# A mixture of experts on one core: gathers three experts ahead, hidden transposes ahead of the down products, second blocks turned and multiplied last

## The chip, the cores and the metric

The kernel runs on one core of a Trainium2 chip. The metric is the time of one execution on the device in microseconds (us); the time before is the median of 3 runs. A trace of one execution tells what each engine did: TensorE (PE; its weight loads are PEld), VectorE (DVE), ScalarE (ACT), GpSimd (POOL) and SyncE (SP), which issues the weight loads.

## The reference

The block is one decoder layer: a mixer (state space and pooling branches), then a mixture of experts over 512 tokens of width 1024, and a final norm. The change is in the experts. Each token picks 8 of 64 experts; each expert is a gated unit of width 256; a shared expert is added. Cut to what matters:

```python
u = modulate(rmsnorm(h), sh2, sc2)                      # 512 x 1024, float32
top_e, wts = routed(sigmoid(u @ w_router))              # 8 experts and weights for each token
for e in range(64):                                     # tokens of e in blocks of 128
    xb = u[tokens_of(e)]
    hid = silu(xb @ we_gate[e]) * (xb @ we_up[e])       # 1024 -> 256
    routed[tokens_of(e)] += (hid @ we_down[e]) * w      # 256 -> 1024
h = h + g2 * (routed + shared)
return rmsnorm(h, final_norm_g)
```

## The kernel before, in words

The expert stage (`experts`) is one loop over 64 experts, unrolled. How many tokens an expert has is known only at run time, so each engine loads the counts into registers and branches. There are three kinds. A light expert (up to 64 tokens, `LIGHT`) uses the float32 weights as they are. A heavy one (65 to 128) splits its weights into a high and a low float32r part (`split`, lines 45 and 46: a ScalarE cast to `wh` and a VectorE subtraction to `wl`) and makes three products for each (lines 61 to 63, `mm3`). An expert with over 128 tokens has a second block, worked like a heavy one. `by_count` chooses light or heavy, `if_heavy` runs a body for heavy ones, `if_two` for those with a second block. A branch is a unit for the semaphores: who waits for something written in a branch waits for the end of that branch on the engine.

For expert e the work is spread over several iterations:

- Index: `onehot` (line 851, VectorE) and `slot_product` (line 858, `ixp`, TensorE) make the token list of expert e + 4; `slot_numbers` reads it out.
- Rows: `fetch` and `fetch_over` gather the token rows into `xg` by an indirect DMA that GpSimd issues (line 885); `scatter` (line 1044) adds the results into `Y` in the same way.
- Turn: `turn_in` transposes gathered rows by TensorE into the two buffers `xt` (line 899); `turn_out` copies them out as a high part `xh` (line 909, ScalarE) and a low part `xl` (line 910, VectorE); a light expert has one copy, `xf`.
- Products: `products` makes gate and up into `gu` (lines 61 to 63, light: 976) and then `hid` (line 999 on VectorE, light: 1185 on ScalarE).
- Hidden: `hidden_in` transposes `hid` into `ht` (line 1008); `hidden_out` copies it out as `hh` (1014) and `hl` (1015); light: `hT`.
- Down: `downs` multiplies by the down weights into the two buffers `yo` (lines 61 to 63, light: 985) and copies to `yl` (1040, light: 988). It runs one iteration late: iteration e has the down products of e - 1.

The loop stands under `manual_schedule`: on each engine the instructions run in the order in which the code is written. In iteration e that is: gathers for e + 2; split of the first weight half of e + 1 (`gu0w`); products of e; products of its second block, if any (`second_products`); transposes of e + 1 (`turns`, `turned`), and in `turned`, for a heavy e + 1, the split of its second weight half (`gu1w`); the transposes of the second block of e + 1 (`next_second`); down products of e - 1; hidden of e; hidden and down products of the second block of e (`second_down`); scatters; weight loads for e + 2. The eight weight buffers are used in a ring, so a load waits on SyncE until a buffer's last reader is through; for the second half and the down weights of e + 2 that is the down product of e - 1.

Of the kernel before, what the change touches and what calls it, by code (L numbers as in the profile page):

```python
# [11 lines left out]
F32 = mybir.dt.float32  # L12
# [11 lines left out]
NT = 4  # L24
# [827 lines left out]
    return oh  # L852


def slot_product(k, ps, oh, vv, b):

    for t in range(NT):
        k.nc.tensor.matmul(ps[:, b, 0:5], oh[:, t, b, :], vv[:, t, :], start=t == 0, stop=t == NT - 1)


# [41 lines left out]
def turn_out(k, halves, x, full=None):  # L902

    nc = k.nc
    for hf, pv in enumerate(halves):
        ks = slice(hf * 4, hf * 4 + 4)
        if full is not None:
            nc.scalar.copy(full[:, ks, :], pv)
        nc.scalar.copy(x[0][:, ks, :], pv)  # L909
        nc.vector.tensor_sub(x[1][:, ks, :], pv, x[0][:, ks, :].bitcast(F32))  # L910
    return x


def turn(k, src, x, full=None):
    halves = turn_tiles(k)
    turn_in(k, src, halves)
    return turn_out(k, halves, x, full)
# [157 lines left out]
def experts(k, shared):  # L1075
# [79 lines left out]
    def by_count(e, engines, light, heavy):  # L1155

        if e == 0:
            heavy()
        elif e < E:
            with tc.If(count(e, engines) <= LIGHT) as small:  # L1160
                light()
            with small.Else():
                heavy()
# [32 lines left out]
    def turned(e, halves):  # L1196

        if e == E:
            return
        def light():  # L1200
            for hf, pv in enumerate(halves):
                nc.scalar.copy(k.xf[:, hf * 4:hf * 4 + 4, :], pv[:, :, :LIGHT])

        def heavy():
            turn_out(k, halves, k.xT[e % 2])
            gu[e][1].split(k, k.gu1w)

        by_count(e, both, light, heavy)

    def downs(e):  # L1210
        if e < 0:
# [6 lines left out]

        by_count(e, every, lambda: down_light(k, k.hT, dn[e], y, w), heavy)

    def hidden_turned(e, hid):
        ps = hidden_in(k, hid)

        def light():
            nc.scalar.activation(k.hT, ps[:, :, :LIGHT], AF.Silu)
            nc.vector.tensor_mul(k.hT, k.hT, ps[:, :, LIGHT:])  # L1226

        by_count(e, both, light, lambda: hidden_out(k, ps, k.hx[e % 2]))

    with tc.manual_schedule():  # L1230
        fetch_over(0)
        fetch_over(1)
        if_two(0, lambda: turn(k, k.xg[3], k.xT[1]))
        for e in range(E):
            fetch(e + 2)
            fetch_over(e + 2)
            onehot(e + 4)
            for i in (e, e + 1):
                if i < E:
                    for engines in (every, both):  # L1240
                        count(i, engines)
            if_heavy(e + 1, both, lambda: gu[e + 1][0].split(k, k.gu0w[(e + 1) % 2]))
            hid = products(e)
            hid1, halves = hidden(k), turn_tiles(k)
            slots = slot_tile(k, 2) if e + 4 < E else None

            def turns():
                if e + 1 < E:
                    turn_in(k, xg[e + 1], halves)

            def second_products():
                gate_act(k, gate_up_mm(k, k.xT[(e + 1) % 2], gu[e]), hid1)
                turns()

            def index_part(b):
                if e + 4 < E:
                    slot_product(k, slots, oh[e + 4], k.V[:, :, e + 4, :], b)

            def next_second():
                index_part(0)  # L1260
                turn(k, k.xg[3 + (e + 1) % 2], k.xT[e % 2])

            def second_down():
                ps = turn_tiles(k)[0].rearrange("p q t -> p (q t)")[:, :2 * P].rearrange("p (j t) -> p j t", j=2)
                hidden_in(k, hid1, ps)
                index_part(1)
                hidden_out(k, ps, k.hx[2])
                for n in range(2):
                    down(k, k.hx[2], dn[e], n, k.xg[2], idx[e][1][:, 1:2])

            if_two(e, second_products, turns)
            turned(e + 1, halves)
            if_two(e + 1, next_second, lambda: index_part(0))
            downs(e - 1)
            hidden_turned(e, hid)
            if_two(e, second_down, lambda: index_part(1))
            if e > 0:
                first(e - 1, lambda n: scatter(k, idx[e - 1], 0, k.yl[(e - 1) % 2], (e - 1) % 2, n))
            second(e, lambda n: scatter(k, idx[e], 1, k.xg[2], e % 2, n))
            load(e + 2)  # L1280
            if e + 4 < E:
                idx[e + 4] = slot_numbers(k, slots, 2)
        e = E - 1
        downs(e)
        first(e, lambda n: scatter(k, idx[e], 0, k.yl[e % 2], 1, n))
        part = k.part = [token_pair(k, k.Y[0], t) for t in (0, 2)]
        for t in range(NT):
            eng = (nc.vector, nc.gpsimd)[t % 2]
            y, h = (u[t // 2][:, t % 2, :] for u in (part, k.hs2))
            eng.tensor_mul(y, y, k.rows[:, 0, :])  # L1290
            eng.tensor_add(h, h, y)  # L1291
# [183 lines left out]
```

## Time and profile before

| what | value |
|---|---|
| median of 3 runs | 1673.15 us (1671.15 to 1684.17) |
| the profiled execution's own time | 1673.0 us |
| its span, first to last instruction | 1671.3 us |
| mean granted TensorE clock, share of full | 0.947 |
| TensorE busy, share of the span | 88% |
| VectorE, ScalarE, GpSimd | 61%, 45%, 22% |
| HBM traffic over the span | 206 GB/s |

Busy is what an engine's instructions cover; a wait is idle time ahead of an instruction, put down to what ended it. "ACTq" or "DVEq" is a sequencer of that engine that signals without work, for instance in passing a branch; "issue" is idle time in which nothing that the profile shows was waited for.

### The profile page before, as it was taken

Reading aid. Unit: us, or ns where it says so; the run is one execution under the profiler, and the core shown is the slowest. Engines: PE = TensorE matmul, PEld = TensorE weight load, DVE = VectorE, ACT = ScalarE, POOL = GpSimd, SP = SyncE. Lnnn points to the kernel's source line nnn. Section 1 sums busy time; section 2 is a strip of 40 time slices with the busy share of each in tenths; the row PEclk is TensorE's granted clock in tenths of the full one; section 3 lists DMA queues with packets and bytes.
Section 4 is the critical chain, followed back from the end, with each engine's and each line's share of the span. In section 5 each row is a group of like instructions: output and inputs, shape, how many; then the busy total and the mean of one; then the engine's idle time right before and its main releaser. Section 6 shows DMA issues by size and latency. Waiting matters only on the chain. (4 is left out here: it accounts for less than half of the span.)

```text
span 1671.3 us, 25992 instructions
## 1 busy us (share of the span) xinstructions
PE 1475.4 (88%) x8084; PEld 1156.2 (69%) x8084; DVE 1011.8 (61%) x1744; ACT 745.2 (45%) x1027; POOL 370.3 (22%) x312
## 2 busy tenths in 40 slices
PE   5999999999999999999898888898798888887970
PEld 5888788788888778888675666566576665665640
DVE  6889778778877974558743354545436453355326
ACT  3465546454434223325544455444536454355332
POOL 5201101002010111220122322322324222221226
PEclk7999999999999999999999999899899989898995
DMA  9442433243333236236738778958889999898974
GB/s 288 122 126 76 138 102 121 76 126 101 107 105 117 82 114 233 87 115 227 294 113 285 252 235 289 329 189 258 282 251 313 324 329 318 287 325 273 297 288 151
DMA packets 152127, 340.32 MB, mean 204 GB/s; under 512 B 15816, under 2 KB 94832, under 8 KB 142272
## 3 DMA queue, kind: packets, MB, share of 16 engines
q1 hardware_dynamic: 135888, 294.94, 51.8%
q0 software_dynamic: 15408, 40.23, 9.4%
q8 instruction: 118, 1.93, 0.5%
q10 hardware_dynamic: 576, 2.10, 0.3%
q14 instruction: 137, 1.12, 0.2%
HBM read 314.00 MB, written 31.01 MB: 206 GB/s over the span
## 5 line engine op out<-in xcount | busy, mean ns | idle before, releaser
L46 DVE TENSOR_TENSOR wl<-raw,wh 128x2048 fp32r<-128x2048 f32 x114 | 273.5, 2404 | 100.0 <-ACT wh L45 88.4
L45 ACT CAST wh<-raw 128x2048 fp32r<-128x2048 f32 x114 | 216.6, 1906 | 140.3 <-PE mm L62 65.7
L1044 POOL DMA_INDIRECT Y<-yl,idx x64 | 108.2, 1691 | 481.8 <-ACT yl L988 271.9
L61 PE MATMUL mm<-uh,wh 128*128 128x512 f32 x432 | 171.7, 397 | 1.9 <-ACT zs L285 1.9
L63 PE MATMUL mm<-uh,wl 128*128 128x512 f32 x432 | 170.4, 395 | 0.0
L62 PE MATMUL mm<-ul,wh 128*128 128x512 f32 x432 | 169.8, 393 | 0.0
L899 PE MATMUL xt<-ident,xg 128*128 128x128 f32 x632 | 97.2, 300 | 58.2 <-issue 18.6
L899 PEld LDWEIGHTS xt<-ident,xg 128*128 128x128 f32 x632 | 84.9, 196 | 77.7 <-issue 48.9
L976 PE MATMUL gu<-raw,xf 128*64 128x256 f32 x1056 | 125.9, 387 | 6.1 <-DMA raw<-in_we_up_dram 3.5
L885 POOL DMA_INDIRECT xg<-u2d,idx x75 | 93.5, 1247 | 117.5 <-DVE oh L851 36.4
L46 DVE TENSOR_TENSOR pair<-raw,pair 128x2048 fp32r<-128x2048 f32 x33 | 75.0, 2290 | 58.2 <-ACT pair L45 49.7
L976 PEld LDWEIGHTS gu<-raw,xf 128*64 128x64 f32 x1056 | 77.2, 138 | 42.6 <-issue 7.2
L61 PE MATMUL gu<-wh,xh 128*128 128x512 f32 x256 | 103.1, 403 | 1.0 <-ACT xh L909 0.6
L62 PE MATMUL gu<-wl,xh 128*128 128x512 f32 x256 | 101.9, 398 | 0.7 <-DVEq L1169 0.7
L63 PE MATMUL gu<-wh,xl 128*128 128x512 f32 x256 | 101.3, 396 | 0.0
L1226 DVE TENSOR_TENSOR hT<-hT,ht 128x128 f32<-128x128 f32 x33 | 9.5, 288 | 146.8 <-ACTq L1169 142.5
L61 PEld LDWEIGHTS mm<-uh,wh 128*128 128x128 f32 x432 | 81.6, 189 | 20.4 <-ACT zs L285 2.3
L63 PEld LDWEIGHTS mm<-uh,wl 128*128 128x128 f32 x432 | 81.6, 189 | 17.7 <-issue 0.9
L62 PEld LDWEIGHTS mm<-ul,wh 128*128 128x128 f32 x432 | 81.5, 189 | 16.8 <-issue 0.4
L45 ACT CAST pair<-raw 128x2048 fp32r<-128x2048 f32 x33 | 62.1, 1903 | 61.7 <-DMA raw<-in_we_gate_dram 22.8
L985 PE MATMUL yo<-raw,hT 128*64 128x512 f32 x264 | 75.5, 695 | 3.5 <-DMA raw<-in_we_gate_dram 2.0
L327 DVE SCALAR_TENSOR_TENSOR cv<-mm,cw,cv 128x511 f32<-128x511 f32 (+2 forms) x90 | 66.6, 741 | 2.1 <-ACT cv L324 1.8
(354 smaller groups left out, 3336.8 us busy)
## 6 DMA issues: line engine op xcount, KB each, us to landing
raw<-in_we_gate_dram SPq DMA_DIRECT2D x124, 512.0 KB
raw<-in_we_up_dram SPq DMA_DIRECT2D x124, 512.0 KB
raw<-in_we_down_dram SPq DMA_DIRECT2D x62, 1024.0 KB
raw<-in_w_in_dram SPq DMA_DIRECT2D x27, 1024.0 KB
raw<-in_w_ada_dram SPq DMA_DIRECT2D x16, 1024.0 KB
big<-in_w_ada_dram SPq DMA_DIRECT2D x16, 512.0 KB
raw<-in_w_in_dram SPq DMA_DIRECT2D x16, 512.0 KB
raw<-in_w_br_ssd_dram SPq DMA_DIRECT2D x8, 1024.0 KB
```

What stands on the lines that cost most here:

```text
L45: nc.scalar.copy(h, raw)
L46: nc.vector.tensor_sub(l, raw, h.bitcast(F32))
L61: nc.tensor.matmul(out, sh, mh, start=first, stop=False)
L62: nc.tensor.matmul(out, sh, ml, start=False, stop=False)
L63: nc.tensor.matmul(out, sl, mh, start=False, stop=last)
L327: nc.vector.scalar_tensor_tensor(cv[:, sft:], ps[:, :T - sft], k.cw[:, j * 32 + blk:j * 32 + blk + 1], cv[:, sft:], op0=ALU.mult, op1=ALU.add)
L885: k.nc.gpsimd.indirect_dma_start(out=xg[:n], out_offset=None, in_=k.u2d, bounds_check=T - 1, oob_is_err=False, in_offset=bass.IndirectOffs ...
L899: k.nc.tensor.transpose(pv[:, q, :], xv[:, hf * 4 + q, :], k.ident)
L976: nc.tensor.matmul(ps[s * LIGHT:(s + 1) * LIGHT, :256], x[:, kk, :], w[:, s, kk % 4, :], start=kk == 0, stop=kk == NK - 1)
L985: nc.tensor.matmul(ps[n * LIGHT:(n + 1) * LIGHT, :], x[:, j, :], unit.raw[:, j * D + n * 512:j * D + n * 512 + 512], start=j == 0, stop=j ...
L1044: k.nc.gpsimd.indirect_dma_start(out=k.Y[acc], out_offset=bass.IndirectOffsetOnAxis(ap=idx[0][:n, b:b + 1], axis=0), in_=y[:n], in_offset= ...
L1226: nc.vector.tensor_mul(k.hT, k.hT, ps[:, :, LIGHT:])
```

## The change

In iteration e the gathers are for e + 3 and stand at the end of the iteration, ahead of the scatters; those for expert 2 stand ahead of the loop. The transposes of the hidden of e (`hidden_in`) come right behind the transposes of e + 1, and those of the second block's hidden behind them in a conditional of their own (`second_turned`), into a `gu` buffer, with its `hidden_out`. The split `gu1w` leaves `turned` and gets a conditional of its own behind that. Then come the down products of e - 1, `hidden_out` of e, only then the second rows of e + 1 (`next_second`), and last the down products of the second block of e. The index product of block 0 is cut in two pieces.

```diff
-def slot_product(k, ps, oh, vv, b):
-
-    for t in range(NT):
+def slot_product(k, ps, oh, vv, b, tiles=range(NT)):
+
+    for t in tiles:
@@ turned
-        def heavy():
-            turn_out(k, halves, k.xT[e % 2])
-            gu[e][1].split(k, k.gu1w)
-
-        by_count(e, both, light, heavy)
+        by_count(e, both, light, lambda: turn_out(k, halves, k.xT[e % 2]))
@@ hidden_turned
-    def hidden_turned(e, hid):
-        ps = hidden_in(k, hid)
-
+    def hidden_turned(e, ps):
@@ the loop
+        fetch(2)
+        fetch_over(2)
         for e in range(E):
-            fetch(e + 2)
-            fetch_over(e + 2)
             onehot(e + 4)
...
+            def second_turned():
+                ps = k.gu.tile([P, 512], F32, name="gu", tag="gu")[:, :2 * P].rearrange("p (j t) -> p j t", j=2)
+                hidden_in(k, hid1, ps)
+                index_part(0, (0, 1))
+                hidden_out(k, ps, k.hx[2])
 
             def next_second():
-                index_part(0)
                 turn(k, k.xg[3 + (e + 1) % 2], k.xT[e % 2])
+                index_part(0, (2, 3))
 
             def second_down():
-                ps = turn_tiles(k)[0].rearrange("p q t -> p (q t)")[:, :2 * P].rearrange("p (j t) -> p j t", j=2)
-                hidden_in(k, hid1, ps)
                 index_part(1)
-                hidden_out(k, ps, k.hx[2])
                 for n in range(2):
                     down(k, k.hx[2], dn[e], n, k.xg[2], idx[e][1][:, 1:2])
 
             if_two(e, second_products, turns)
             turned(e + 1, halves)
-            if_two(e + 1, next_second, lambda: index_part(0))
+            ps = hidden_in(k, hid)
+            if_two(e, second_turned, lambda: index_part(0, (0, 1)))
+            if_heavy(e + 1, both, lambda: gu[e + 1][1].split(k, k.gu1w))
             downs(e - 1)
-            hidden_turned(e, hid)
+            hidden_turned(e, ps)
+            if_two(e + 1, next_second, lambda: index_part(0, (2, 3)))
             if_two(e, second_down, lambda: index_part(1))
+            fetch(e + 3)
+            fetch_over(e + 3)
```

How the instructions stand on three engines. On TensorE in the middle of the loop, from the end of the heavy down products (`yo<-pair,hh`, into `yo`) to the transposes of the hidden, before:

```order
L61 MATMUL yo<-pair,hh_6172 128x512
L62 MATMUL yo<-pair,hh_6172 128x512
L63 MATMUL yo<-pair,hl_6173 128x512
L1160 UNCONDITIONAL_BRANCH
L1008 MATMUL ht<-ident,hid 128x128 x2
L1160 UNCONDITIONAL_BRANCH
L1086 UNCONDITIONAL_BRANCH
L1116 UNCONDITIONAL_BRANCH
L1169 COMPARE_AND_BRANCH
L1008 MATMUL xt<-ident,hid 128x128 x2
L858 LDWEIGHTS oh
```

And now, from the transposes of the next expert's rows (`xt<-ident,xg`) on:

```order
L899 MATMUL xt<-ident,xg_5333 128x128 x8
L1169 UNCONDITIONAL_BRANCH
L1008 MATMUL ht<-ident,hid 128x128 x2
L1160 UNCONDITIONAL_BRANCH
L1116 UNCONDITIONAL_BRANCH
L1169 COMPARE_AND_BRANCH
L1008 MATMUL gu<-ident,hid 128x128 x2
L858 LDWEIGHTS oh
```

The transposes into `ht` moved from behind the down products to right behind the transposes of the next rows, and the second block's follow them, into `gu`.

On VectorE at the end of `turned` for a heavy expert, from the low parts of the turned rows (`xl`) to the hidden, before:

```order
L910 TENSOR_TENSOR xl_6489<-xt,xh_6488 128x512 x2
L46 TENSOR_TENSOR wl<-raw,wh 128x2048
L1160 UNCONDITIONAL_BRANCH
L1169 COMPARE_AND_BRANCH
L910 TENSOR_TENSOR xl_6491<-xt,xh_6490 128x512 x2
L1169 UNCONDITIONAL_BRANCH x2
L1160 COMPARE_AND_BRANCH
L1160 UNCONDITIONAL_BRANCH x2
L1160 COMPARE_AND_BRANCH
L1226 TENSOR_TENSOR hT<-hT,ht 128x128
```

And now:

```order
L910 TENSOR_TENSOR xl_6491<-xt,xh_6490 128x512 x2
L1160 UNCONDITIONAL_BRANCH
L1116 UNCONDITIONAL_BRANCH
L1169 COMPARE_AND_BRANCH
L1015 TENSOR_TENSOR hl_6177<-gu,hh_6176 128x256
L1169 UNCONDITIONAL_BRANCH x2
L1176 COMPARE_AND_BRANCH
L46 TENSOR_TENSOR wl<-raw,wh 128x2048
L1176 UNCONDITIONAL_BRANCH x2
L1160 COMPARE_AND_BRANCH
L1160 UNCONDITIONAL_BRANCH x2
L1160 COMPARE_AND_BRANCH
```

The weight split (`wl<-raw,wh`) left the branch of the turned rows; the second block's hidden (`hl<-gu`) stands ahead of it, and the second rows' `xl` are gone from this place.

On GpSimd where one iteration ends, from the scatter of a second block (`Y<-xg`) to the next gather (`xg<-u2d`), before:

```order
L1044 DMA Y_60<-xg_5334,idx 512x1024
L1127 UNCONDITIONAL_BRANCH
L1126 ISA
L1126 UNCONDITIONAL_BRANCH
L1116 COMPARE_AND_BRANCH x3
L885 DMA xg_5333<-u2d,idx 16x1024
```

And now, from the last gather of a second block to the first block's scatter (`Y<-yl`):

```order
L885 DMA xg_5336<-u2d,idx 128x1024
L1127 UNCONDITIONAL_BRANCH
L1126 ISA
L1126 UNCONDITIONAL_BRANCH
L1116 COMPARE_AND_BRANCH x3
L1044 DMA Y_61<-yl,idx 512x1024
```

The gathers moved from behind both scatters to ahead of them.

## Rows read from the trace of the kernel before

**Rows 1.** Busy time of the engines in five stretches of the expert stage, then the granted TensorE clock, the DMA engines' share and GB/s.

```profile
840.00:1007.00 167.00, 147.59 (x816) 110.47 (x814) 67.34 (x130) 71.92 (x107) 40.71 (x29) 0.94 0.70 225
1007.00:1130.00 123.00, 109.18 (x660) 79.01 (x659) 56.90 (x116) 60.33 (x85) 34.69 (x25) 0.94 0.81 271
1130.00:1266.00 136.00, 114.80 (x648) 85.01 (x646) 61.44 (x114) 63.54 (x88) 38.30 (x23) 0.92 0.82 263
1266.00:1501.00 235.00, 200.91 (x1237) 143.85 (x1234) 114.11 (x234) 114.75 (x161) 65.25 (x45) 0.93 0.93 318
1501.00:1628.00 127.00, 101.78 (x585) 70.42 (x583) 47.08 (x84) 55.41 (x80) 28.43 (x20) 0.93 0.84 289
```

**Rows 2.** TensorE's waits from 840 to 1007 us: who waited for whom, us in total, how often, the longest.

```profile
PE xt L899 <- ACT wh L45: 8.1, 3, 4.5
PE yo L61 <- ACT hh L1014: 4.7, 5, 1.4
PE xt L1008 <- DVEq L1169: 2.7, 1, 2.7
PE xt L899 <- issue: 2.1, 1, 2.1
```

**Rows 3.** The same from 1007 to 1130 us.

```profile
PE xt L899 <- issue: 3.4, 1, 3.4
...
PE yo L61 <- ACT hh L1014: 2.0, 2, 1.2
...
PE xt L899 <- ACT xh L909: 1.1, 1, 1.1
```

**Rows 4.** The same from 1130 to 1266 us; the last row is the one wait there of `xt L899` for "issue", as the view in order of time has it (start, duration, instruction, and in brackets the idle time ahead of it).

```profile
PE xt L899 <- ACT wh L45: 6.0, 1, 6.0
PE xt L899 <- DVE xl L910: 5.7, 1, 5.7
PE yo L61 <- ACT hh L1014: 2.9, 3, 1.4
...
1233.12 1.94 PE L899 MATMUL xt<-ident,xg 128*128 128x128 f32 x8 [2.06 <-issue]
```

**Rows 5.** The same from 1266 to 1501 us.

```profile
PE ht L1008 <- DVEq L1160: 10.0, 2, 6.2
PE ht L1008 <- DVEq L1169: 7.7, 4, 3.4
PE xt L899 <- DMA xg<-u2d,idx: 6.9, 5, 2.2
```

**Rows 6.** The same from 1501 to 1628 us.

```profile
PE xt L899 <- issue: 6.9, 2, 5.4
PE xt L1008 <- DVEq L1169: 2.6, 1, 2.6
PE ht L1008 <- DVEq L1160: 2.4, 1, 2.4
...
PE xt L899 <- ACT wh L45: 1.3, 1, 1.3
```

**Rows 7.** SyncE's own waits ahead of the weight loads, 840 to 1620 us, in the same columns.

```profile
SPq L946 <- PE yo L61: 243.5, 27, 26.7
SPq L946 <- PE yo L985: 144.8, 23, 14.0
```

**Rows 8.** The gathers among the DMA issues: how many, and the median us from issue to landing.

```profile
xg<-u2d,idx POOLq DMA_INDIRECT x75, 9.2
```

**Rows 9.** Instructions in order of time around 890 us, a light expert ahead of a two-block one: start, duration, engine, line, operation, names, shape, count, and in brackets the idle time ahead and what ended it.

```profile
892.84 2.29 DVE L46 TENSOR_TENSOR wl<-raw,wh 128x2048 fp32r<-128x2048 f32 x1 [3.68 <-ACT wh L45]
...
896.86 1.94 PE L899 MATMUL xt<-ident,xg 128*128 128x128 f32 x8 [4.47 <-ACT wh L45]
...
898.74 3.53 PE L985 MATMUL yo<-raw,hT 128*64 128x512 f32 x8
```

**Rows 10.** The same around 918 us, the end of a two-block expert: light down products of the expert before, the first down product of the second block, and the first product of the next expert.

```profile
914.87 1.94 PE L985 MATMUL yo<-raw,hT 128*64 128x512 f32 x8
...
918.96 0.51 PE L61 MATMUL yo<-pair,hh 128*128 128x512 f32 x1 [1.39 <-ACT hh L1014]
...
921.98 1.30 PE L976 MATMUL gu<-raw,xf 128*64 128x256 f32 x10
```

**Rows 11.** The same around 1285 us, a heavy expert ahead of a heavy one.

```profile
1280.00 0.42 DVE L1015 TENSOR_TENSOR hl<-ht,hh 128x256 fp32r<-128x256 f32 x1 [0.60 <-DVEq L1169]
...
1282.24 1.05 PE L899 MATMUL xt<-ident,xg 128*128 128x128 f32 x8
...
1284.09 4.49 DVE L46 TENSOR_TENSOR wl<-raw,wh 128x2048 fp32r<-128x2048 f32 x2 [2.10 <-ACT wh L45]
...
1288.50 0.41 DVE L999 TENSOR_TENSOR hid<-hid,gu 128x256 f32<-128x256 f32 x1
...
1289.06 0.47 PE L1008 MATMUL ht<-ident,hid 128*128 128x128 f32 x2 [2.33 <-DVEq L1169]
```

**Rows 12.** The same around 1140 us, a heavy expert ahead of a two-block one.

```profile
1136.19 1.13 PE L899 MATMUL xt<-ident,xg 128*128 128x128 f32 x8 [0.17 <-DMA xg<-u2d,idx]
...
1141.49 0.41 DVE L999 TENSOR_TENSOR hid<-hid,gu 128x256 f32<-128x256 f32 x1
...
1143.14 1.94 PE L899 MATMUL xt<-ident,xg 128*128 128x128 f32 x8 [5.74 <-DVE xl L910]
```

**Rows 13.** The same around 1319 us, the first of a heavy expert's down products.

```profile
1318.79 0.79 PE L61 MATMUL yo<-wh,hh 128*128 128x512 f32 x1 [3.08 <-issue]
```

More of the change, by code (lines that the diff above doesn't have):

```diff
@@ L1253, in second_products, with index_part @@
                 turns()
-            def index_part(b):
+            def index_part(b, tiles=range(NT)):
                 if e + 4 < E:
-                    slot_product(k, slots, oh[e + 4], k.V[:, :, e + 4, :], b)
+                    slot_product(k, slots, oh[e + 4], k.V[:, :, e + 4, :], b, tiles)
+            def second_turned():
[3 more added lines that the diff above has]
+                hidden_out(k, ps, k.hx[2])
             def next_second():
-                index_part(0)
                 turn(k, k.xg[3 + (e + 1) % 2], k.xT[e % 2])
+                index_part(0, (2, 3))
             def second_down():
-                ps = turn_tiles(k)[0].rearrange("p q t -> p (q t)")[:, :2 * P].rearrange("p (j t) -> p j t", j=2)
-                hidden_in(k, hid1, ps)
                 index_part(1)
-                hidden_out(k, ps, k.hx[2])
                 for n in range(2):
```

## The prediction

> **What bounds the kernel now.** I read the waits first, since the change touches the expert stage alone: it runs to about 1628 us, and what stands before it (mixer, router) and behind it (final norm) is the same. Five stretches of it [rows 1] show TensorE busy 80 to 89% of the time and the DMA engines 70, 81, 82, 93 and 84%. Neither is saturated on average; each idles while it waits for the other. The kinds of expert explain the pattern: the weights of any expert are 3 MB, but a two-block one (over 128 tokens) has twice the matmuls of a heavy one (65 to 128) and a light one (up to 64) far fewer. Ten two-block experts stand between 840 and 1266: five, two and three in the first stretches, as the counts of `yo L61` behind `hh L1014` tell [rows 2 to 4]; one comes behind 1501. There the DMA has slack; from 1266 to 1501 it has least.
>
> The views of TensorE's waits by stretch [rows 2 to 6] then say what it stood for. Before 1266 it is nearly all `xt L899` (transposes of gathered rows), behind `wh L45`, `xl L910` or "issue", and `yo L61` (down products of a second block). After 1266 it is `ht L1008` (transposes of the first block's hidden), behind a VectorE sequencer. SyncE's own waits [rows 7] show who paces the loads: its weight loads waited 243.5 + 144.8 us for TensorE to get to a down product, so a later down product means a later load.
>
> **The change, part by part.**
>
> *Second rows turned later.* `next_second` goes from ahead of the down products to behind them and behind `hidden_turned`. Its transposes need the two `xt` buffers back, and so far these came back only at the end of `turned`'s branch, which held the split of the second weight half (`gu1w`). Around 890 TensorE stood 4.47 us for that, until 896.86 [rows 9]. With the split in a conditional of its own and 2 to 3 us of down products in between, I cost this wait at zero. The stall doesn't vanish with it, because of the next part.
>
> *Hidden transposes ahead of the down products.* `hidden_in` for the first block now comes right behind the next expert's transposes. It waits for `hid` L999 on VectorE or, in a light expert, for VectorE to get past the branch; the splits of the next expert's weights, and of this one's down weights, are ahead of that in VectorE's queue. What hid this so far was the down product of the previous expert: 1.94 us for a light one (914.87), 3.0 us for twelve wide matmuls (918.96 to 921.98) [rows 10]. Three cases bound the new wait. Around 890 VectorE's split ends at 895.13, and TensorE was free from 896.86 - 4.47 = 892.4: 2.8 of the 4.5 us stay [rows 9]. Around 1137 `hid` is ready at 1141.90 and TensorE was free from 1137.4: 4.5 of 5.7 us stay [rows 12]. Around 1283, in a run of heavy experts, the transposes end at 1283.3 and `hid` at 1288.9: TensorE waited 2.33 us after its down products [rows 11], and now waits 5.6 us ahead of them. So a place that waits already loses its down product as cover, 1.94 to 3.0 us, and the loads that ride on the down product [rows 7] shift with it. A lone heavy expert has a new wait between 0 and 2 us.
>
> *Second hidden turned early, second down products last.* So far `yo L61` waited for `hh L1014`, 1.39 us at 918.96 [rows 10]. Now `hidden_out` of that block runs beside the first down products, and this is zero; if that cover were too short (ScalarE has the `gu1w` split ahead of the copies that free `yo`), part of the 1.39 us would come back where a heavy expert follows. The transposes take a `gu` buffer instead of an `xt` one, so the 2.7 and 2.6 us of `xt L1008` [rows 2, 6] go as well. `index_part` issues the same eight matmuls, in three pieces instead of two.
>
> *Gathers three ahead.* On GpSimd a gather, and the second block's, now stand ahead of the scatter of e - 1 and of the second block's scatter, and no longer behind them; these scatters come later by the issue of the gathers, and the buffers that they free are wanted an expert or two later. SyncE's queue keeps its order. A gather takes 9.2 us to land [rows 8], and TensorE's waits for it are 6.9 us in the fourth stretch [rows 5]. It pays only where no `ht` wait stands right behind: between 0 and 6.9 us, I take 2.
>
> *Two more conditionals* per expert on VectorE and ScalarE, one on TensorE. Before `hl L1015` VectorE shows a gap of 0.60 us that holds several [rows 11]; I take 0.3 us each, 0.6 per expert, and count it for ten heavy experts in whose stretch VectorE sets the pace: 6 us, between 0 (hidden everywhere) and 62 x 0.6 = 37.
> [...]
>
> **The sum**, by stretch, removed less new:
> - 840 to 1007: removed 8.1 + 2.1 + 2.7 + 4.7 = 17.6 [rows 2]; new `ht` waits at three light experts ahead of two-block ones, 2.8 by rows 9 and 1 each for the others (between 0 and 2.8). Net -13.
> - 1007 to 1130: removed 3.4 + 1.1 + 2.0 = 6.5 [rows 3], new 2 in the same way (0 to 2.8). Net -5.
> - 1130 to 1266: removed 6.0 + 5.7 + 2.1 + 2.9 = 16.7 [rows 4]; of the two long ones 4.5 each stays [rows 12], and 2.5 at light experts. Net -5.
> - 1266 to 1501: no two-block expert. The 10.0 + 7.7 us of `ht` waits, in six places [rows 5], stay, and each place loses some 2 us of cover: +12; gathers -2. Net +10.
> - 1501 to 1628: removed 6.9 + 2.6 + 1.3 = 10.8 [rows 6], of which 4 stay as `ht` wait and 1 for a gather. Net -6.
> - Conditionals: +6.
>
> Together -13. Against the profiled execution of 1673.0 us (span 1671.3; the median of the runs, 1673.15, is the same) that is **1660 us**. Left out, as likely in both directions: after a stall the light down product that takes 1.94 us at 914.87 took 3.53 us at 898.74 [rows 9, 10], so a stall gone or a new one is worth up to 1.6 us more.
>
> **Rivals.**
> *The loads absorb the new waits.* If the weights set the pace in the fourth stretch whatever TensorE does, the +10 and the +6 fall into time that TensorE would wait anyway. For it: the DMA share of 0.93 leaves 16 us of 235 [rows 1]. Against it: SyncE waited 243.5 us for TensorE [rows 7]. It gives -13 - 5 - 5 - 2 - 6 = -31: 1642.
> *The gains are absorbed too.* If a faster two-block expert only reaches the next missing weights sooner, the first three stretches keep a quarter of their 23 us and the rest is even: 1668 to 1673. For it: in the second and third stretch the DMA share is 0.81 and 0.82 already. Against it: the stretch with five two-block experts has the lowest DMA share, 0.70 [rows 1].
> *The `ht` wait takes over: slower.* If about every second of the 62 experts, those that are heavy or stand ahead of a heavy one, waits 2 us more at `ht L1008`, that is 60 us, and 6 for conditionals, against the 52 us removed in the four stretches with second blocks [rows 2 to 4, 6]: +14, and a few more for late loads, 1690. It decides from a mean of (52 - 6) / 30 = 1.5 us. Rows 11 speak for it, the lone heavy experts against.
> [...]
> [...]
> *The change doesn't do what it says* could be so for the gathers alone: issued earlier, landing no earlier. That takes the 2 us from the sum: 1662.
>
> **How the numbers follow.** Forecast 1660, from 1650 to 1667, with the gathers' case in it: 0.44. Loads absorb the new waits, around 1642: 0.27. Gains absorbed, or fetch stops, 1668 to 1674: 0.19. The `ht` wait takes over, around 1690: 0.10. A measurement of this kernel tells about 1% from no change, 16.7 us. Faster by more is all of the second case and a fifth of the first, 0.36; slower by more is somewhat over half of the last, 0.06; within 1%: 0.58. The range leaves out the part of the fast case below 1640 and of the slow one above 1686.
>
> **What would show it.** `xt L899` behind `wh L45` (8.1 + 6.0 + 1.3) and `yo L61` behind `hh L1014` (4.7 + 2.0 + 2.9) should nearly leave the waits; `ht L1008` behind VectorE's sequencer should rise from the 20 us of rows 5 and 6 to 45 or 60; the first three stretches should shorten by some 23 us together, the fourth lengthen by some 10. The forecast is wrong if `ht L1008` stays near 20, if the fourth stretch shortens, or if the first three keep their length with a DMA share as before.

## The result, and the profile after

The changed kernel takes 1698.3 us (median of 4 runs, 1694.8 to 1700.9) against 1673.0 for the kernel before: a ratio of 1.0136 with a 95% interval from 1.0088 to 1.0184. It is slower by some 25 us, and the prediction (1660, range 1640 to 1686) was wrong in sign and in range. The profiled execution took 1700.9 us, with a span of 1699.1 us, 27.8 longer than before, and a mean granted clock of 0.943. One execution of a later kernel (the one with the split back, 1711.6 us) was in a slower state, over 1.5% above that kernel's fastest, and is left out of its median.

The five stretches of [rows 1], cut at the start of the same experts' products. Columns: stretch, length, busy time of TensorE, its weight loads, VectorE, ScalarE and GpSimd, granted clock, DMA share, GB/s.

```profile
837.00:998.40 161.40, 147.85 (x843) 111.72 (x841) 72.23 (x140) 76.55 (x111) 41.18 (x30) 0.98 0.73 237
998.40:1126.50 128.10, 108.81 (x663) 78.45 (x660) 57.84 (x116) 61.29 (x86) 31.80 (x25) 0.95 0.80 263
1126.50:1258.30 131.80, 115.27 (x646) 85.10 (x644) 63.63 (x115) 63.80 (x87) 32.79 (x23) 0.95 0.85 273
1258.30:1519.90 261.60, 211.85 (x1243) 143.99 (x1240) 112.48 (x232) 115.38 (x161) 62.92 (x45) 0.90 0.85 284
1519.90:1655.00 135.10, 102.95 (x579) 68.35 (x576) 47.03 (x84) 54.80 (x79) 24.70 (x19) 0.89 0.80 269
```

Against the lengths of [rows 1] that is -5.6, +5.1, -4.2, +26.6 and +8.1 us. Only the first and the third became shorter. The fourth, with heavy and light experts alone, carries nearly the whole loss. Its DMA share fell from 0.93 to 0.85, that is 219 us of transfers in 235 before and 222 in 261.6 now: the added time is not time of the transfers. Its clock fell from 0.93 to 0.90, and TensorE's busy time for nearly the same number of matmuls rose from 200.9 to 211.9 us. Over the five stretches together, 30 us longer, TensorE is busy 12.5 us more and idle 17.5 us more.

TensorE's waits after, over the whole expert stage (820 to 1665 us): who waited for whom, us in total, times, longest.

```profile
PE ht L1008 <- DVEq L1160: 63.4, 15, 10.4
PE ht L1008 <- DVEq L1169: 29.4, 15, 4.9
PE gu L976 <- DMA raw<-in_we_up_dram: 8.3, 7, 2.3
PE yo L61 <- ACT yl L988: 6.9, 6, 1.5
```

All that stands in [rows 2 to 4, 6] for `xt L899` behind `wh L45`, `xl L910` and issue, and for `yo L61` behind `hh L1014`, is gone. In its place TensorE waits for the hidden rows (`ht L1008`), 30 times for 92.8 us. SyncE's waits, the answer to [rows 7], grew at light down products from 144.8 to 169.8 us:

```profile
SPq L946 <- PE yo L61: 244.2, 28, 21.6
SPq L946 <- PE yo L985: 169.8, 22, 12.5
```

Instructions in order of time at a heavy expert ahead of a heavy one, the kind of place of [rows 11]: start, duration, engine, line, operation, names, and in brackets the idle time ahead.

```profile
1277.81 2.29 DVE L46 TENSOR_TENSOR wl<-raw,wh 128x2048 fp32r<-128x2048 f32 x1
...
1280.01 0.42 DVE L999 TENSOR_TENSOR hid<-hid,gu 128x256 f32<-128x256 f32 x1
...
1280.58 0.47 PE L1008 MATMUL ht<-ident,hid 128*128 128x128 f32 x2 [2.50 <-DVEq L1169]
...
1281.86 0.63 PE L62 MATMUL yo<-pair,hh 128*128 128x512 f32 x1
...
1282.28 0.63 PE L63 MATMUL yo<-pair,hl 128*128 128x512 f32 x1
...
1285.23 0.40 PE L61 MATMUL yo<-pair,hh 128*128 128x512 f32 x1
...
1285.46 0.40 PE L62 MATMUL yo<-pair,hh 128*128 128x512 f32 x1
```

Two prices are to be seen. TensorE stands 2.50 us until VectorE is through with a weight split and `hid`. Then come the down products, which it could have worked in that time, and they run slow: they start 0.42 us apart until 1284.84, and 0.23 from 1285.23 on. The granted clock of that stretch, and of the same twelve products in the kernel before, which there stand ahead of the wait:

```profile
1281.30:1286.60 5.30, 5.12 (x20) 3.97 (x21) 3.05 (x3) 1.24 (x3) 0.00 (x0) 0.68 0.12 39
```

```profile
1283.30:1286.70 3.40, 3.08 (x16) 2.17 (x12) 2.61 (x2) 3.06 (x4) 0.00 (x0) 1.00 1.03 363
```

The 0.68 has two parts: 0.56 from 1281.30 to 1285.00 and 1.00 from 1285.20 on. In the kernel before the clock is 1.00 throughout, and the products from 1284.04 to 1286.35 start 0.23 us apart, like the last ones here.

The longest wait, in the fifth stretch, a light expert ahead of a heavy one:

```profile
1530.65 1.90 ACT L45 CAST pair<-raw 128x2048 fp32r<-128x2048 f32 x1 [9.91 <-DMA raw<-in_we_up_dram]
1532.45 0.37 ACT L1185 COPY hid<-gu 128x256 f32<-128x256 f32 x1
1532.58 2.29 DVE L46 TENSOR_TENSOR pair<-raw,pair 128x2048 fp32r<-128x2048 f32 x1 [9.83 <-ACT pair L45]
...
1535.07 0.67 PE L1008 MATMUL ht<-ident,hid 128*128 128x128 f32 x2 [10.40 <-DVEq L1160]
1535.83 3.68 PE L985 MATMUL yo<-raw,hT 128*64 128x512 f32 x8
```

ScalarE and VectorE stand at the split of the next expert's weights, whose load has not landed; the copy of `hid` is queued behind that split, the `ht` transposes wait until VectorE, through with its part of the split at 1534.87, has passed the branch in which `hid` is written (the sequencer at L1160), and the down products behind them, on which the next loads wait, wait too. They take 3.68 us, against 1.94 at 914.87 in [rows 10]. The stretches of these two, after and before, in the columns of the table above (granted clock 0.50 and 1.00):

```profile
1535.80:1539.50 3.70, 3.67 (x9) 0.91 (x9) 3.07 (x3) 1.14 (x1) 0.00 (x0) 0.50 0.59 219
```

```profile
914.87:916.80 1.93, 1.93 (x12) 0.55 (x9) 0.00 (x0) 0.40 (x2) 0.00 (x0) 1.00 0.09 34
```

The sums of both prices, from the groups of TensorE's instructions over the expert stage: busy us and mean ns of the light down products (L985) and of the `ht` transposes, then the idle time ahead of them. Before:

```profile
L985 PE MATMUL yo<-raw,hT 128*64 128x512 f32 x264 | 75.5, 695 | 3.5 <-DMA raw<-in_we_gate_dram 2.0 <-ACTq L1169 0.7 <-issue 0.7
...
L1008 PE MATMUL ht<-ident,hid 128*128 128x128 f32 x124 | 28.4, 312 | 23.0 <-DVEq L1160 15.3 <-DVEq L1169 7.7
```

After:

```profile
L985 PE MATMUL yo<-raw,hT 128*64 128x512 f32 x264 | 86.4, 785 | 6.4 <-DMA raw<-in_we_gate_dram 2.1 <-issue 1.5 <-PEq L1169 0.7
...
L1008 PE MATMUL ht<-ident,hid 128*128 128x128 f32 x124 | 29.0, 318 | 91.0 <-DVEq L1160 63.4 <-DVEq L1169 26.3 <-ACTq L1176 0.8
```

So 68 us more of waiting at `ht`, and 10.9 us more for the same 264 products. These 264 are eight for each of 33 light experts: now 15 of the 33 take 3.1 to 3.7 us at a granted clock of 0.50 to 0.61, where 9 took over 3 us before (eight of them at 0.54 to 0.62); all others take 1.94.

### The profile page after: what moved, and what is told of

The parts are those of the page before. It is cut to its first block, busy times and chain, and to the rows that moved or that the text cites. A ratio compares the mean times of both kernels' runs of the same rounds, so it can differ in the third digit from the quotient of the medians.

```text
span 1699.1 us, 26579 instructions
## 1 busy us (share of the span) xinstructions
PE 1487.4 (88%) x8084; PEld 1154.3 (68%) x8084; DVE 1012.8 (60%) x1744; ACT 747.0 (44%) x1027; POOL 355.0 (21%) x312
## 5 line engine op out<-in xcount | busy, mean ns | idle before, releaser
L45 ACT CAST wh<-raw 128x2048 fp32r<-128x2048 f32 x114 | 216.3, 1904 | 147.1 <-PE mm L62 66.4
L61 PE MATMUL mm<-uh,wh 128*128 128x512 f32 x432 | 171.9, 398 | 1.9 <-ACT zs L285 1.9
L62 PE MATMUL mm<-ul,wh 128*128 128x512 f32 x432 | 169.8, 393 | 0.0
L1044 POOL DMA_INDIRECT Y<-yl,idx x64 | 94.5, 1477 | 311.5 <-ACT yl L988 186.5
L976 PE MATMUL gu<-raw,xf 128*64 128x256 f32 x1056 | 128.3, 386 | 15.7 <-DMA raw<-in_we_up_dram 8.3
L1008 PE MATMUL ht<-ident,hid 128*128 128x128 f32 x136 | 31.9, 319 | 94.1 <-DVEq L1160 63.4
L61 PE MATMUL gu<-wh,xh 128*128 128x512 f32 x256 | 101.8, 398 | 1.0 <-ACT xh L909 1.0
L62 PE MATMUL gu<-wl,xh 128*128 128x512 f32 x256 | 100.6, 393 | 0.5 <-DVE wl L46 0.5
L899 PEld LDWEIGHTS xt<-ident,xg 128*128 128x128 f32 x632 | 80.7, 193 | 26.2 <-issue 22.5
L61 PEld LDWEIGHTS mm<-uh,wh 128*128 128x128 f32 x432 | 81.5, 189 | 20.3 <-ACT zs L285 2.3
L62 PEld LDWEIGHTS mm<-ul,wh 128*128 128x128 f32 x432 | 81.6, 189 | 16.9 <-issue 0.4
L985 PE MATMUL yo<-raw,hT 128*64 128x512 f32 x264 | 86.4, 785 | 6.4 <-DMA raw<-in_we_gate_dram 2.1
L899 PE MATMUL xt<-ident,xg 128*128 128x128 f32 x632 | 89.1, 284 | 1.2 <-PE gu L976 0.9
L1008 PEld LDWEIGHTS ht<-ident,hid 128*128 128x128 f32 x136 | 21.6, 205 | 100.7 <-ACTq L1169 73.5
```

The source lines that it names most:

```text
L45: nc.scalar.copy(h, raw)
L61: nc.tensor.matmul(out, sh, mh, start=first, stop=False)
L62: nc.tensor.matmul(out, sh, ml, start=False, stop=False)
L899: k.nc.tensor.transpose(pv[:, q, :], xv[:, hf * 4 + q, :], k.ident)
L976: nc.tensor.matmul(ps[s * LIGHT:(s + 1) * LIGHT, :256], x[:, kk, :], w[:, s, kk % 4, :], start=kk == 0, stop=kk == NK - 1)
L985: nc.tensor.matmul(ps[n * LIGHT:(n + 1) * LIGHT, :], x[:, j, :], unit.raw[:, j * D + n * 512:j * D + n * 512 + 512], start=j == 0, stop=j ...
```

## The experiments

All times are medians; ratios, with 95% intervals, are to the kernel before on the same chip. Not all kernels ran on the same chip; the kernel before took 1672.2 to 1673.7 us on each.

### Which part of the change costs

Four kernels, one line or one part each. First, the changed kernel with the hidden transposes where they were:

```diff
-            ps = hidden_in(k, hid)
             if_two(e, second_turned, lambda: index_part(0, (0, 1)))
             if_heavy(e + 1, both, lambda: gu[e + 1][1].split(k, k.gu1w))
             downs(e - 1)
+            ps = hidden_in(k, hid)
             hidden_turned(e, ps)
```

> The changed kernel with one line moved back: the transposes of the first block's hidden stand behind the down products of the expert before again; all else as changed. Theory A (TensorE now waits for the hidden rows with the down products still undone, and the weight loads that ride on those down products come later): the 93 us of `ht L1008` behind VectorE's sequencer fall back to some 25, the stretch of heavy experts to about 237 us from 261.6, and the time is 1640 to 1655, under both kernels. Theory B (the gathers ahead of the scatters on GpSimd cost it): 1690 to 1700. Theory C (the added conditionals cost it, on VectorE, ScalarE and TensorE): 1685 to 1695.

Measured: 1644.1 us, 0.9834 (0.9797 to 0.9870). One line turns the loss into a gain of 30 us. Its groups:

```profile
L985 PE MATMUL yo<-raw,hT 128*64 128x512 f32 x264 | 63.9, 604 | 4.1 <-DMA raw<-in_we_gate_dram 1.5 <-DVEq L1169 1.2 <-ACTq L1169 0.6
...
L1008 PE MATMUL ht<-ident,hid 128*128 128x128 f32 x124 | 29.4, 322 | 45.4 <-DVEq L1160 34.8 <-DVEq L1169 9.8 <-issue 0.7
```

The wait at `ht` fell by half, to 45.4 us and not to the 25 expected, and the light down products are 22.5 us faster than in the changed kernel: all 33 groups of eight take 1.94 us.

Second, the other way round, that one move on the kernel before:

```diff
             turned(e + 1, halves)
+            ps = hidden_in(k, hid)
             if_two(e + 1, next_second, lambda: index_part(0))
             downs(e - 1)
-            hidden_turned(e, hid)
+            hidden_turned(e, ps)
```

> The kernel before with one line moved: the transposes of the first block's hidden stand ahead of the down products of the expert before; nothing else is changed. Theory A: slower than both, 1700 to 1725, as the waits for second blocks stay and those for the hidden rows come on top. Theory B and theory C: within 8 us of the kernel before, 1665 to 1681.

Measured: 1714.1 us, 1.0231 (1.0190 to 1.0272): 40 us slower by this move alone. Its idle time at `ht` is 80.4 us, 57 more than before, while the waits at `xt L899`, 57.9 us before, are 22.3: part of the waiting only moved to the earlier step, without any move of the second rows.

Third and fourth, the gathers and a conditional:

```diff
-        fetch(2)
-        fetch_over(2)
         for e in range(E):
+            fetch(e + 2)
+            fetch_over(e + 2)
...
-            fetch(e + 3)
-            fetch_over(e + 3)
```

> The changed kernel with the gathers two experts ahead again, at the head of the loop and so behind the last expert's scatters on GpSimd; all else as changed. Theory A: the loss stays, 1695 to 1705. Theory B: 1660 to 1675. Theory C: 1695 to 1705.

```diff
-        by_count(e, both, light, lambda: turn_out(k, halves, k.xT[e % 2]))
+        def heavy():
+            turn_out(k, halves, k.xT[e % 2])
+            gu[e][1].split(k, k.gu1w)
+
+        by_count(e, both, light, heavy)
...
-            if_heavy(e + 1, both, lambda: gu[e + 1][1].split(k, k.gu1w))
```

> The changed kernel with the split of the second weight half back inside the branch that turns the next expert's rows out, so one conditional fewer on VectorE and ScalarE; the other moves stay. That puts this split ahead of VectorE's passing of nothing that the hidden transposes wait for, so theory A: 1690 to 1705, the loss stays. Theory C (one conditional of two is gone): 1675 to 1685. Theory B: as changed, 1695 to 1702.

Measured: 1694.5 us, 1.0123 (1.0082 to 1.0165), and 1698.4, 1.0130 (1.0075 to 1.0184). Neither is told from the changed kernel. In the first, the wait for gathers was back:

```profile
PE xt L899 <- DMA xg<-u2d,idx: 12.0, 9, 2.6
```

but the idle time at `ht` was 79.3 us instead of 91.0: the 12 us that the gathers had saved were waited for one step later. Theory A held in three of the four and missed its range by half a microsecond in the kernel with the gathers back; B (GpSimd) and C (conditionals) fell.

### Why the order costs: late weights, or VectorE's own work

Two readings were left. A1: the split waits for weights, and down products that come late make later loads later, a ring that feeds itself. A2: VectorE's own work makes `hid` late, and the down products are lost as its cover. Four kernels (the two with quarter loads leave out three quarters of the weights of experts 4 to 63, so their times are a measure only):

```diff
-            if_heavy(e + 1, both, lambda: gu[e + 1][0].split(k, k.gu0w[(e + 1) % 2]))
             hid = products(e)
...
             turned(e + 1, halves)
+            if_heavy(e + 1, both, lambda: gu[e + 1][0].split(k, k.gu0w[(e + 1) % 2]))
```

> The changed kernel with one line moved: the split of the next expert's first weight half, which waits for its load, stands behind the turning out of the next expert's rows on VectorE and ScalarE, no longer ahead of this expert's products. That the order of TensorE costs the time is settled by the two kernels before; open is by what. Theory A1 (the hidden rows come late because VectorE stands at that split for weights): `ht L1008` behind VectorE's sequencer falls from 93 us to under 45, and the time to 1650 to 1670. Theory A2 (VectorE's own work is what is late, and only the down product as its cover is lost): `ht` stays over 70 us, 1685 to 1705. A third way: the split is now late for the next expert's products, which wait at `gu L61` for more than `ht` gives back: above 1705.

```diff
-                load_gu(k, a.we_gate[0, e], a.we_up[0, e], gu[e])
-                load_down(k, a.we_down[0, e], dn[e])
+                load_gu(k, a.we_gate[0, e], a.we_up[0, e], gu[e], 1)
+                load_down(k, a.we_down[0, e], dn[e], 512)
...
-        k.nc.sync.dma_start(rv[:, 0], gv[:, hf * 4:hf * 4 + 4, :])
+        k.nc.sync.dma_start(rv[:, 0, :m], gv[:, hf * 4:hf * 4 + m, :])
```

> The changed kernel, but the loads of experts 4 to 63 move a quarter of each weight's bytes into the same buffers (the rest of a buffer keeps what was there), so that no weights are late; every other instruction is the same. Theory A1 (the waits are for weights): well under the next kernel plus 20 us. Theory A2: 45 to 60 us above the next kernel, as with full loads (1698 less 1644).

> The kernel with quarter loads and the hidden transposes behind the down products of the expert before again. TensorE's busy time sets it: 1500 to 1590 by both theories. Theory A1: less than 20 us under the kernel with quarter loads. Theory A2: 45 to 60 us under it.

```diff
+    def ring(e):
+        g = [k.raws[i] for i in (0, 1, 3, 4, 6)]
+        d = [k.raws[i] for i in (2, 5, 7)]
+        n = 2 * (e - 1)
+        gu[e], dn[e] = [Unit(k, g[n % 5]), Unit(k, g[(n + 1) % 5])], Unit(k, d[(e - 1) % 3])
...
+        if e < E:
+            ring(e)
+            sure(e, lambda: half(e, 0))
+        if 1 < e <= E:
+            sure(e - 1, lambda: load_down(k, a.we_down[0, e - 1], dn[e - 1]))
+        if e < E:
+            sure(e, lambda: half(e, 1))
```

> The changed kernel with the eight weight buffers parted into five for gate and up and three for down, and SyncE's order first half of expert e + 2, down weights of e + 1, second half of e + 2. No load of an expert then waits for the down products that now stand behind the hidden transposes: it waits for down products of one expert earlier. Theory A1 with the ring of late down products and late loads as its cause: 1655 to 1675, and SyncE's waits for `yo` fall by more than half. Theory A2: 1690 to 1702.

Measured: split behind 1657.0 us, 0.9895 (0.9857 to 0.9933); quarter loads 1616.7, 0.9655 (0.9619 to 0.9691); the same with the hidden transposes back 1561.2, 0.9335 (0.9303 to 0.9367); parted buffers 1638.9, 0.9790 (0.9752 to 0.9829). The first and the last spoke for A1, the last even past its range. With the split behind, the waits at `ht` nearly leave, and others come at the products that now wait for the split:

```profile
PE gu L62 <- DVEq L1169: 29.4, 23, 1.8
...
PE ht L1008 <- DVEq L1169: 11.0, 12, 2.2
```

The pair with quarter loads spoke against A1 as the whole cause, and more plainly. In the changed order ScalarE's splits waited 90.7 us for weights with full loads and wait 28.8 with a quarter, and yet the order costs 1616.7 - 1561.2 = 55 us, as with full loads (54). Groups of the quarter-load kernel in the changed order, and with the hidden transposes back:

```profile
L988 PE MATMUL yo<-raw,hT 128*64 128x512 f32 x264 | 76.4, 703 | 7.0 <-issue 3.3 <-PEq L1172 1.9 <-DMA raw<-hsd 0.6
L1011 PE MATMUL ht<-ident,hid 128*128 128x128 f32 x124 | 27.9, 307 | 44.6 <-DVEq L1172 26.0 <-DVEq L1163 12.1 <-ACTq L1172 4.3
```

```profile
L988 PE MATMUL yo<-raw,hT 128*64 128x512 f32 x264 | 63.9, 604 | 4.3 <-ACTq L1172 1.3 <-DVEq L1172 1.2 <-ACT xh L909 1.0
L1011 PE MATMUL ht<-ident,hid 128*128 128x128 f32 x124 | 27.9, 307 | 7.6 <-DVEq L1172 7.1 <-DVEq L1163 0.3
```

Of those 55 us the two prices make 49.5: 37.0 of waiting at `ht`, and 12.5 for the same light down products (703 ns each in the mean against 604; the granted clock from 1260 to 1500 us is 0.95 in the first kernel and 0.99 in the second). With full loads the same two prices are 45.6 and 22.5 us; the runs do not say why the totals still agree. In the parted kernel two things are new, the two rings and SyncE's order of loads; no run tells one from the other. In the ring of eight it is the load of a second half that takes a buffer read by down products, and the down weights, which take one of a first half, stand behind that load in SyncE's queue. What the parted buffers give had to be tried in the other orders:

> Parted weight buffers (five for gate and up, three for down) together with the hidden transposes behind the down products of the expert before; the other parts of the change as they are. Theory A2 as the quarter loads left it (VectorE's queue costs some 55 us with or without late weights, so the costs add): 1639 less 54, some 1580 to 1600. Theory A1 (what the rings gave was the ring of late down products and late loads, which this order does not have to the same degree): 1625 to 1645.

> The kernel before with the parted weight buffers and nothing else. Theory A2 (late weights cost each order about the same): 1605 to 1630, some 60 us as for the changed kernel. Theory A1 (the loads hurt the changed order above all): 1655 to 1675.

> The kernel before with loads of experts 4 to 63 of a quarter of the bytes (the rest of a buffer keeps what was there). Theory A2: late weights cost 82 us in the changed kernel and 83 with the hidden transposes back; the same here gives 1585 to 1595, and the change without late weights is 20 to 30 us slower as with them. Theory A1: 1600 to 1625, so that the change loses nothing once weights are never late.

Measured: parted buffers with the hidden transposes back 1592.5 us, 0.9523 (0.9494 to 0.9553); on the kernel before 1632.2, 0.9764 (0.9725 to 0.9804); quarter loads on the kernel before 1598.1, 0.9544 (0.9498 to 0.9589). The first is in A2's range. The second lies 2 us above A2's and far under A1's. The third lies between the two ranges, but the change still loses there. With them the table is full (us):

| order | loads as they were | parted buffers | quarter loads |
|---|---|---|---|
| before | 1673 | 1632 | 1598 |
| changed | 1698 | 1639 | 1617 |
| changed, hidden back | 1644 | 1592.5 | 1561 |
| cost of the hidden transposes ahead | 54 | 46 | 55 |
| gain of the rest of the change | 29 | 40 | 37 |

The three quarters of the loads cost the orders 75, 82 and 83 us, the parted buffers give back 41, 59 and 52, and the early hidden transposes cost 46 to 55 in all three columns. A smaller load also leaves the gathers less traffic (in the changed order 114 GB/s from 1260 to 1500 us with quarter loads, 284 without), so the last column is what loads cost in all, not only by late weights. The change as a whole loses 19 us even there (1616.7 less 1598.1). The changed kernel with parted buffers and the hidden transposes back is the fastest of those that load all weights, 4.8% under the kernel before. Its wait at `ht`:

```profile
PE ht L1008 <- DVEq L1191: 7.6, 8, 1.9
```

### What is left of the split's place

> The changed kernel with both: the split of the next expert's first weight half behind the turned rows, and the hidden transposes behind the down products of the expert before. If the split costs because it stands ahead of the hidden rows with nothing to cover it, the down products cover it here and moving it gives nothing more or takes some: 1640 to 1665, with `gu L62` behind VectorE for 20 to 30 us as in the kernel with the split behind alone. If the two are separate gains: 1600 to 1625.

> The changed kernel with quarter loads (experts 4 to 63 load a quarter of the bytes, the rest of a buffer keeps what was there) and the split of the next expert's first weight half behind the turned rows. Theory A3 (the split costs by its own time on VectorE, ahead of the hidden rows): it takes away most of the 55 us that the order costs with quarter loads, as it took 41 of 54 with full ones: 1570 to 1585, and `ht` behind VectorE falls from 41 to under 20 us. Theory A1 (the split costs by its wait for weights, which quarter loads take away): it gives under 10 us, 1608 to 1620.

> Parted weight buffers, the hidden transposes behind the down products of the expert before, and the split of the next expert's first weight half behind the turned rows; the rest as in the change. As with full loads the split's place should give nothing once the down products cover it: 1585 to 1600, beside 1592.5 without this move. Under 1580 would say that the split's place is worth something by itself.

Measured: 1644.3 us, 0.9823 (0.9781 to 0.9865), no gain once the down products cover the split; 1616.0 with quarter loads, 0.9679 (0.9647 to 0.9710), no gain either, beside 1616.7; and 1622.6 with parted buffers and the hidden transposes back, 0.9695 (0.9668 to 0.9721), a loss of 30 where none was expected: its products now wait for the split (`gu L62` behind VectorE's sequencer, 29.1 us), and there was little waiting at `ht` left to save. So the 41 us that the split's place was worth in the changed kernel hang on its wait for weights (A1's half of the story), and A3, in which its own time is saved, fell as far as the time goes. Waits of the quarter-load kernel with the split behind:

```profile
PE gu L62 <- DVEq L1172: 25.3, 21, 1.8
PE ht L1011 <- DVEq L1172: 13.3, 14, 2.4
PE yo L61 <- ACT yl L991: 11.5, 6, 3.0
```

The idle time at `ht` did fall, from 44.6 to 15.9 us, but the next products (`gu L62`) wait 25.3 us for the split that has become late. VectorE's own work had only changed the place where TensorE meets it; of what was tried, only work for TensorE in the meantime, the down products, hides it.

### The other parts alone

> The kernel before with the next expert's second rows turned behind the down products and the hidden rows, and the split of the second weight half in a conditional of its own; hidden transposes, gathers and second block's hidden as before. By the rows of the kernel before, `xt L899` behind `wh L45`, `xl L910` and issue leaves some 30 to 35 us: 1640 to 1650. If the gain is the second block's hidden or the gathers instead: 1668 to 1675.

> The kernel before with the second block's hidden turned ahead of the down products into a `gu` buffer, and nothing else. By its rows the 9.6 us of `yo L61` behind `hh L1014` and 5.3 us of `xt L1008` go: 1655 to 1665. If VectorE's queue takes it back, as it did for the first block's hidden: 1670 to 1690.

> The kernel before with one more conditional per expert on TensorE, VectorE and ScalarE, with nothing in either branch, ahead of the down products of the expert before. The kernel with the second block's hidden turned early alone was 24 us slower and has exactly this conditional. If the conditional is that cost: 1685 to 1700, some 0.4 us for each of 62 experts. If the cost is in the moved transposes: 1670 to 1677.

> The kernel with parted weight buffers and the hidden transposes behind the down products, with the second block's hidden turned at the head of the second down products again (still in a `gu` buffer), so that one conditional per expert goes on three engines. If a conditional costs some 0.4 us: 1568 to 1580. If its cost hides once the weights come in time, and the cover of the early second hidden is lost: 1592 to 1605.

Measured: second rows later alone 1662.4 us, 0.9936 (0.9914 to 0.9959), 10 us faster where 22 to 32 were expected. Its trace shows `xt L899` behind `wh L45` at 1.5 us, as forecast, but the second block's hidden, which still needs the `xt` buffers and now comes after the second rows, waits:

```profile
PE xt L1008 <- DVEq L1169: 17.7, 9, 3.5
```

Second hidden early alone: 1696.1 us, 1.0141 (1.0104 to 1.0178), 24 us slower where 8 to 18 faster was expected. An empty conditional per expert on three engines: 1672.3, 0.9999 (0.9987 to 1.0011), nothing. The fastest kernel with its second hidden late again: 1600.4, 0.9575 (0.9562 to 0.9587), 8 us slower than with it early, though it has one conditional fewer; the wait that the early place had covered is back:

```profile
PE yo L61 <- ACT hh L1014: 15.6, 11, 2.1
```

So the two moves belong together: alone they give 10 us and cost 24, together (with the gathers, whose share is not told from nothing) they give 30. For the first alone the trace says why, the buffers on which the second block's hidden waits. Why the second alone costs 24 us stays open. An empty conditional in that place costs nothing, and the trace shows short waits ahead of the light down products, 20.6 us of them where the kernel before has 3.5, and 25 us ahead of the heavy ones (the groups `yo<-pair,hh` and `yo<-wh,hh` of L61) where it has 16: together 26 us more, about what it lost, but not why.

## Why the prediction was wrong

- **What leaves.** Right: `xt L899` behind `wh L45` and `yo L61` behind `hh L1014` are gone, all 52 us of the four stretches with second blocks. But what left was not all gain: with the hidden transposes back, where these waits are nearly gone too, the change is worth 30 us in the time, not 52, and the idle time at `ht` is 45.4 us instead of 23.0. Part of the waiting for VectorE had only moved.
- **What comes: the term that failed.** "A place that waits already loses its down product as cover, 1.94 to 3.0 us" was the right mechanism, counted at too few places: the trace has 30 waits at `ht`, the kernel before had 9. By stretch the sum comes to 4.8, 3.4, 13.0, 29.7 and 6.4 us, 57.3 in all, with the waits that stood there before (1.4 and 1.5 us of them, in the second and third stretch, are not in its rows); the trace has 7.5, 15.7, 13.0, 34.2 and 19.3, 89.7 in all. The second and the fifth stretch are off by 12 and 13 us, with one wait of 9.4 and one of 10.4 us: light experts ahead of a heavy one whose weights were late. The sum had "1 each for the others", bounded by 2.8 from the one place of [rows 9]; that bound did not hold.
- **What was left out.** A stall's effect on the next down product, "up to 1.6 us", was left out "as likely in both directions". It was not: the move puts the down products right behind the wait, and 15 of 33 instead of 8 ran at about half the clock (0.50 to 0.62). They took 10.9 us more than before and 22.5 more than with the hidden transposes back. In the fourth stretch, where the sum of `ht` waits was only 4.5 us off, TensorE's busy time rose by 10.9 us at a clock of 0.90 instead of 0.93; the sum has no term for that.
- **Conditionals.** Put at +6; the empty one, in the order before, changed the time by less than 3 us either way (0.9987 to 1.0011), and one fewer in the changed order gave nothing that can be told from noise.
- **The sum, mended.** -13, and 32 for the `ht` waits (89.7 against 57.3), and 11 for the slower light products, less 6 for the conditionals: +24, beside 27.8 measured in the span. The other 4 us are not assigned. Of the signs that it named, the waits that leave and the rise at `ht` came, the latter beyond its 45 to 60 us; the first three stretches shortened by 5 us together and not by 23, and the fourth lengthened by 27 and not by 10.
- **The rivals.** "The `ht` wait takes over", 1690, was what happened, 8 us short: 30 places with 68 us more in all, 2.3 us each, over its threshold of 1.5. That its number came so near is partly luck, as it counted 6 us for conditionals that cost nothing and had no slower products. It had a chance of 0.10, because lone heavy experts were taken as evidence against it. The three places looked at [rows 9, 11, 12] were all forecast to wait 2.8 us or more in the new order, though in two of them a longer wait was to go. That should have outweighed an assumption about places not looked at. "The loads absorb the new waits" failed: the fourth stretch grew by 27 us. No run shows the "fetch stops" that share a chance with the absorbed gains. What the runs showed in their place is TensorE's waits for "issue" from 820 to 1665 us: 26.6 us in 14 waits before, the longest 5.4, and 5.6 us in 14 after, the longest 1.6; with the added conditionals none is as long as the 3.08 us of [rows 13]. "A few more for late loads" in the slow rival was right in kind only: late loads make some waits long (10.4 us at most, against 3.2 with quarter loads), but the order costs as much without them, as the table shows.

## What to carry to other kernels

Before a step that waits is moved ahead of one that is ready, sum the wait over every place, not over the places that already show one: here TensorE lost the ready work as cover (1698.3 us against 1644.1 with the transposes back), and the down products of 15 of the 33 light experts ran at a granted clock of 0.50 to 0.61, where 8 ran at 0.54 to 0.62 before. To learn whether late loads are the cause, run both orders with a quarter of the bytes; if the difference stays, they are not the whole cause. And try a ring of buffers for each kind of load: in the common ring loads waited for down products (243.5 and 144.8 us in [rows 7]), and two rings with a load order to suit gave each of the three orders 41 to 59 us.

## What the runs showed of the hardware

- A conditional per expert with nothing in it, on TensorE, VectorE and ScalarE, changed the time by a factor of 0.9999 (0.9987 to 1.0011).
- Behind two waits of about the same length the granted clock was not the same: behind the 2.33 us wait of [rows 11] the next products ran at a granted clock of 1.00, as the stretch from 1289.10 to 1293.00 has it, while behind the 2.50 us wait at 1280.58 the granted clock was 0.68 from 1281.30 to 1286.60. Over the stage it matters: the same 264 light down products took 63.9 us in one order and 86.4 in the other, 1.94 us for eight at a granted clock of 1.00 (914.87 of the kernel before) and up to 3.68 at 0.50.
- The gathers' median time from issue to landing was 6.7 us in the changed kernel, against the 9.2 of [rows 8], at nearly the same traffic (203 GB/s over the span, 206 before).
